# Mixing the three dilation groups inside the attention units of one hybrid decoder layer

## The chip, the cores and the metric

One Trainium2 chip, 1 core of it. The metric is device time in microseconds (us) of one launch, the median over runs. Engines: PE (matmuls), PEld (its weight loads), DVE, ACT and POOL (elementwise work), SP (issues every DMA of this kernel, in one queue, in order).

## The reference, cut to what matters

```python
def dilated_attention_branch(q, k, v):
    q, k, v = q.reshape(shp), k.reshape(shp), v.reshape(shp)   # (B, L, 3 groups, 4 heads, 128)
    for gi, (window, dilation) in enumerate(((128, 1), (512, 4), (2048, 16))):
        o, s = dilated_group_attention(q[:, :, gi], k[:, :, gi], v[:, :, gi], window, dilation)
        outs.append(o); lses.append(s)
    alpha = jax.nn.softmax(jnp.stack(lses, axis=0), axis=0)
    y = jnp.sum(alpha[..., None] * outs, axis=0)
    return y.reshape(bsz, L, ATTN_WIDTH)

def reference(x, ...):                                   # L = 2048, D_MODEL = 1024
    h = rmsnorm(x, pre_norm_g); proj = h @ w_in
    u_s, z_s, q, k, v, z_a, g_s, g_a = jnp.split(proj, SPLIT_POINTS, axis=-1)
    y_s = s5_branch(u_s, ...) * jax.nn.silu(z_s)
    y_a = dilated_attention_branch(q, k, v) * jax.nn.silu(z_a)
    merged = jax.nn.sigmoid(g_s) * (y_s @ w_branch_s) + jax.nn.sigmoid(g_a) * (y_a @ w_branch_a)
    return x + rmsnorm(merged @ w_out, post_norm_g)
```

Head slot j (0 to 3) exists in each of the three groups. Its three outputs are mixed with weights that come from the three softmax denominators.

## The kernel before, in words

The normalised input stays in SBUF as a high and a low part (`hhi`, `hlo`), and each column strip of `w_in` (128 columns) is split in the same way when it is loaded: a product is three fp32r passes, hi*hi, hi*lo and lo*hi, 24 matmuls of 512 columns for one bank of PSUM (`proj`, L141). Strips come in pairs (`pair`): four loads of 256 KB into tag `w_raw`, which has 2 buffers, and for each an ACT pass (`w_hi`, L67) and a DVE pass (`w_lo`, L68) into one of two pairs of `w_hi`/`w_lo` tiles. So the next pair can be loaded while PE works on the present one, and split when the pair before that is done with.

The stages in order: input and norm; u; the state-space branch, beside g_s, z_s and v products; its GLU; **attention**; the g_a and z_a strips; the output stage (branch products, merge, `w_out`).

Attention (`unit`) runs 12 units: head slots j = 0 to 3, and in each groups g = 0, 1, 2. A unit projects K and Q for four chunks of 512 positions. In groups 0 and 1 (`banded_chunk`) a chunk has four blocks of 128 queries against two blocks of keys (own and previous), in fp32r with high and low parts; in group 0 the last key block of a chunk is carried into the next chunk's `kh[:, 0]`, `kl[:, 0]` by two POOL copies (L848, L849). A first block without a predecessor still takes 256 columns of keys (`k0:k0+2`), and a third mask block removes the second half. Group 2 (`causal_chunk`) uses plain fp32 with 128 columns. A chunk's unnormalised output goes to DRAM (`numd`), and a unit's row maxima and sums (`statd`) follow when its last chunk is done, after a transpose (`tst`, L866).

After the last unit, `weights_of_groups` reads the statistics of each head slot, on 16 partitions, makes the three factors per position and stores them (`fd`). `combine(j)` then forms y = sum over g of factor*output for a head slot in 12 tiles of 512 positions: two loads each (`cf`: the factor row broadcast to 128 partitions; `cn`: the output), and POOL multiplies and adds. `cf` has 2 buffers, `cn` 3. Two head slots' y stay in SBUF (`cy`) and are the factor of a z_a pair (`silu_pair`). The g_a pairs (`tanh`) stand between: g_a 0-1, g_a 2-3, z_a 0-1, g_a 4-5, z_a 2-3, g_a 6-7. Each pair has 8 banks; a bank is 24 matmuls, an ACT evict into one of two `ev` buffers (`ge`, `ze`), and a store by SP (L699). A pair's weights are free to load before `combine`, from buffers of their own.

The order on each engine is made by a scheduler at build time from its own estimates; at run time every engine, and SP's queue, works strictly in that order.

Of the kernel before, what the change touches and what calls it, by code (L numbers as in the profile page):

```python
# [39 lines left out]
class Builder:  # L40
# [782 lines left out]

    def unit(self, j, g, wp, pool, ev, psum, numd, statd):
        nc = self.nc
# [4 lines left out]
        for c in range(4):  # L830
# [24 lines left out]
            else:  # L855
# [47 lines left out]
    def banded_chunk(self, g, c, carry, qh, ql, kh, kl, vh, vl, prev, st, pool, ev, psum, dst):  # L903
        nc = self.nc
        ph, pl = (pool.tile([128, 8, 128], F32R, name=n) for n in ("ph", "pl"))
        for pair in range(2):
# [3 lines left out]
            for h in range(2):  # L910
                b = 2 * pair + h
                k0 = 1 if b == 0 and not carry else b
                for n, (x, y) in enumerate(((qh, kh), (qh, kl), (ql, kh))):
                    nc.tensor.matmul(s[:, h], x[:, b], y[:, k0 : k0 + 2], start=n == 0, stop=n == 2)  # L914
            for h in range(2):
                b = 2 * pair + h
                first = b == 0 and not carry
                p = self.softmax(s[:, h], self.mask[:, 128:384] if first else self.mask[:, 0:256], 4 * c + b, st, pool)
# [29 lines left out]
        pv(nb[:, 2:4], (vh[:, 2], vl[:, 2]), 5)  # L948
        lo = pool.tile([128, 4, 128], F32, name="nlo")
        if carry:  # L950
            nc.scalar.activation(lo[:, 0:2], na[:, 0::3], AF.Copy)
        else:
            nc.scalar.activation(lo[:, 1], na[:, 3], AF.Copy)
        nc.scalar.activation(lo[:, 2:4], nb[:, 1::2], AF.Copy)
        if carry:
            nc.vector.tensor_tensor(dest[:, 0], blocks(na[:, 2:3])[:, 0], blocks(lo[:, 0:1])[:, 0], op=ALU.add)
        else:
            nc.vector.tensor_copy(dest[:, 0], blocks(na[:, 2:3])[:, 0])
        nc.vector.tensor_tensor(dest[:, 1:3], blocks(nb[:, 0::2]), blocks(lo[:, 1:3]), op=ALU.add)
        nd = psum.tile([128, 2, 128], F32, tag="n", name="nd")  # L960
        pv(nd, (vh[:, 3], vl[:, 3]), 6)
        nc.vector.tensor_tensor(dest[:, 3], blocks(nd[:, 1:2])[:, 0], blocks(lo[:, 3:4])[:, 0], op=ALU.add)
        nc.sync.dma_start(dst, acc)
# [18 lines left out]

    def weights_of_groups(self, j, pool, statd, fd):

        nc = self.nc
        m = pool.tile([16, 6, 128], F32, name="cm")
        nc.sync.dma_start(m, statd[j].rearrange("g s (r i) -> r (g s) i", r=16))
        mx = pool.tile([16, 128], F32, name="cx")
        nc.vector.tensor_tensor(mx, m[:, 0], m[:, 2], op=ALU.max)
        nc.vector.tensor_tensor(mx, mx, m[:, 4], op=ALU.max)  # L990
        e = pool.tile([16, 3, 128], F32, name="ce")
# [3 lines left out]
        t = pool.tile([16, 3, 128], F32, name="ct")  # L995
        nc.vector.tensor_tensor(t, e, m[:, 1::2], op=ALU.mult)
# [3 lines left out]
        for g in range(3):  # L1000
            nc.vector.tensor_tensor(e[:, g], e[:, g], mx, op=ALU.mult)
        nc.sync.dma_start(fd[j].rearrange("g (r i) -> r g i", r=16), e)

    def combine(self, j, pool, numd, fd):

        nc = self.nc
        y = pool.tile([128, SEQ], F32, name="cy", bufs=2)
        for q in range(4):
            qs = slice(512 * q, 512 * q + 512)
            yo = y[:, qs]  # L1010
            for g in range(3):
                f = pool.tile([128, 512], F32, name="cf", bufs=2)
                nc.sync.dma_start(f, fd[j, g : g + 1, qs].to_broadcast([128, 512]))
                n = pool.tile([128, 512], F32, name="cn", bufs=3)
                if g == 0:
                    src = numd[j, 0].rearrange("c p (h x) -> h p c x", h=4)[q]
                    nc.sync.dma_start(n.rearrange("p (c x) -> p c x", c=4), src)
                    vn = n.rearrange("p (c r i) -> p r c i", c=4, r=4)
                    vf, vy = (t.rearrange("p (r c i) -> p r c i", r=4, c=4) for t in (f, yo))
                elif g == 1:  # L1020
                    src = numd[j, 1].rearrange("c p (h x) -> h p c x", h=4)[q]
                    nc.sync.dma_start(n.rearrange("p (c x) -> p c x", c=4), src)
                    vn, vf, vy = n, f, yo
                else:
                    nc.sync.dma_start(n, numd[j, 2, q])
                    vn, vf, vy = n, f, yo
                if g == 0:
                    nc.gpsimd.tensor_tensor(vy, vn, vf, op=ALU.mult)
                else:
                    nc.gpsimd.tensor_tensor(vn, vn, vf, op=ALU.mult)  # L1030
                    nc.gpsimd.tensor_tensor(vy, vy, vn, op=ALU.add)
        return y

# [99 lines left out]
    def run(self, stop=None):  # L1133
        tc, nc, a = self.tc, self.nc, self.a
        with (
# [12 lines left out]
            statd = dp.tile([4, 3, 2, SEQ], F32, name="statd")  # L1148
            fd = dp.tile([4, 3, SEQ], F32, name="fd")
            self.vd = dp.tile([3, SEQ, 512], F32, name="vd")  # L1150
            self.ident = cst.tile([128, 128], F32, name="ident")
# [9 lines left out]
            with tc.tile_pool(name="w", bufs=2, **T) as wp, tc.tile_pool(name="ev", bufs=2, **T) as ev:  # L1161
# [37 lines left out]
                with tc.tile_pool(name="at", bufs=1, **T) as ap:  # L1199
                    self.mask = ap.tile([128, 384], F32, name="mask")  # L1200
# [4 lines left out]
                if stop == "att":  # L1205
                    return

                def emit(banks):
                    for bank in banks:
                        for step in bank:  # L1210
                            step()

                def tanh(c):
                    emit(self.tanh_pair(ev, psum, self.pair(wp, IDX_GA + c, IDX_GA + c + 1), gta[c : c + 2]))

                with tc.tile_pool(name="cb", bufs=1, **T) as cp:
                    for j in range(4):
                        self.weights_of_groups(j, cp, statd, fd)
                    for p in range(2):
                        y = [self.combine(j, cp, numd, fd) for j in (2 * p, 2 * p + 1)]  # L1220
                        if p == 0:
                            tanh(0)
                        tanh(2 + 2 * p)
                        i = IDX_ZA + 2 * p
                        emit(self.silu_pair(ev, psum, self.pair(wp, i, i + 1), ya[2 * p : 2 * p + 2], y))
                if stop == "ya":
                    return
                with tc.tile_pool(name="bs", bufs=1, **T) as bp:
                    tanh(6)
                    wb = [self.weight(bp, wp, "w_raw", n, 4, (0, 512)) for n in ("wbs", "wba")]  # L1230
# [12 lines left out]
def prepare(x, pre_norm_g, w_in, lambda_re, lambda_im, log_dt, b_re, b_im, c_re, c_im, d_skip, w_glu, b_glu,  # L1243
# [14 lines left out]
    own, before = np.where(to <= at, 0.0, NEG), np.where(to >= at, 0.0, NEG)  # L1258
    never = np.full((128, 128), NEG)
    mask = np.concatenate([before, own, never], 1)  # L1260
    diag0 = np.zeros((16, 8, 16))
# [33 lines left out]
```

## Time and profile before

| | us |
|---|---|
| median of 3 runs (2089.51 to 2094.95) | 2092.69 |
| the profiled execution's own time | 2096.55 |
| its span in the trace | 2094.7 |
| PE busy | 2049.4 (98%) |
| DVE busy | 903.0 (43%) |
| ACT busy | 592.3 (28%) |
| POOL busy | 397.8 (19%) |

PE is the engine to watch: it is busy nearly all the time, so what counts is where it is not, and where its granted clock falls from 2.4 to 1.2 GHz. The other engines matter through the waits that they cause. The times inside the span are counted from its start: attention ends near 1446 us, the g_a and z_a strips follow to about 1722 us, then the output stage.

### The profile page before, as it was taken

To read this page: it belongs to the slowest core of one execution; us is meant where nothing else is said; L and a number is where in the kernel's file an instruction comes from. 1 tells how busy PE (TensorE), PEld (TensorE's weight loads), DVE (VectorE), ACT (ScalarE), POOL (GpSimd) and SP (SyncE) were. 2 spreads that over 40 slices of the span, in tenths; PEclk is the share of its full clock that TensorE was granted. 3 is DMA by queue.
4 is the path that set the end of the run, shared out by engine and by line. 5 is a ranking of instruction groups with operands and counts; after the bars stand their busy time and mean duration, and the time that the engine had idled before them with its cause. 6 is when DMAs were issued, how large, how long until landed. Compare 5 with 4: busy or idle time off the path is not lost.

```text
span 2094.7 us, 30801 instructions
## 1 busy us (share of the span) xinstructions
PE 2049.4 (98%) x11668; PEld 1786.1 (85%) x11668; DVE 903.0 (43%) x2261; ACT 592.3 (28%) x1327; POOL 397.8 (19%) x384
## 2 busy tenths in 40 slices
PE   8999999999999999999999999999889999999998
PEld 6788888999999988888888888887777887999997
DVE  6881355555442234324424423434311226544434
ACT  6421122222223234334434333432111124112111
POOL 0002355555521200000000000001636101111111
PEclk9999999999999999999999999999999999999999
DMA  7333333333445421111111121113757246433323
GB/s 247 116 115 140 103 115 113 118 114 113 117 121 174 152 67 57 56 61 51 61 56 56 37 66 51 61 52 118 223 157 230 88 136 201 138 125 116 117 81 101
DMA packets 208372, 231.50 MB, mean 111 GB/s; under 512 B 24864, under 2 KB 142944, under 8 KB 207968
## 3 DMA queue, kind: packets, MB, share of 16 engines
q1 hardware_dynamic: 208224, 229.54, 34.9%
q8 instruction: 91, 1.49, 0.3%
q14 instruction: 57, 0.47, 0.1%
HBM read 146.52 MB, written 74.56 MB: 106 GB/s over the span
## 4 chain that ended last, share of the span: by engine, by line
PE 86%; DMA 7%; DVE 2%; ACT 1%; POOL 1%; issue 1%; SPq 0%; DVEq 0%; ACTq 0%; POOLq 0%
PE proj L141 46%; PE pv L163 13%; PE po L1108 8%; PE br L1089 8%; DMA cf<-fd 2%; PE glu L786 2%; PE s L914 2%; PE nb L940 1%; DMA raw<-in_wout_dram 1%; PE na L940 1%; PE nc L978 1%; PE py L598 1%; POOL cn L1030 1%; PE s L970 1%; PE pd L561 1%
## 5 line engine op out<-in xcount | busy, mean ns | idle before, releaser
L141 PE MATMUL proj<-hhi,w_hi 128*128 128x512 f32 x1664 | 664.6, 400 | 25.4 <-ACT ge L693 15.6
L141 PE MATMUL proj<-hlo,w_hi 128*128 128x512 f32 x1664 | 658.2, 396 | 3.3 <-DVE hlo L68 2.7
L141 PE MATMUL proj<-hhi,w_lo 128*128 128x512 f32 x1664 | 657.5, 395 | 0.0
L141 PEld LDWEIGHTS proj<-hhi,w_hi 128*128 128x128 f32 x1664 | 314.5, 189 | 95.0 <-ACT ge L693 18.4
L141 PEld LDWEIGHTS proj<-hlo,w_hi 128*128 128x128 f32 x1664 | 314.3, 189 | 71.3 <-DVE hlo L74 3.2
L141 PEld LDWEIGHTS proj<-hhi,w_lo 128*128 128x128 f32 x1664 | 314.3, 189 | 64.8
L163 PE MATMUL pv<-w_hi,hhi 128*128 128x256 f32 x768 | 218.8, 285 | 0.0
L163 PE MATMUL pv<-w_hi,hlo 128*128 128x256 f32 x768 | 214.5, 279 | 0.0
L163 PE MATMUL pv<-w_lo,hhi 128*128 128x256 f32 x768 | 214.5, 279 | 0.0
L68 DVE TENSOR_TENSOR w_lo<-w_raw,w_hi 128x512 fp32r<-128x512 f32 (+1 forms) x130 | 107.9, 854 | 195.8 <-ACT w_hi L67 195.3
L163 PEld LDWEIGHTS pv<-w_hi,hhi 128*128 128x128 f32 x768 | 144.5, 188 | 0.6
L163 PEld LDWEIGHTS pv<-w_lo,hhi 128*128 128x128 f32 x768 | 144.4, 188 | 0.6
L163 PEld LDWEIGHTS pv<-w_hi,hlo 128*128 128x128 f32 x768 | 144.4, 188 | 0.0
L898 ACT ACTIVATE p<-p,nm 128x256 f32<-128x256 f32 (+1 forms) x192 | 89.5, 467 | 151.8 <-DVE nm L897 135.7
L892 DVE CUSTOM_DVE_ANT_0 p<-s,mask 128x256 f32<-128x256 f32 (+1 forms) x192 | 68.2, 376 | 147.1 <-PE t L973 68.8
L1092 POOL TENSOR_TENSOR gt<-gt 128x256 f32<-128x256 f32 x64 | 48.7, 763 | 390.6 <-DVE gt L1091 224.7
L67 ACT ACTIVATE w_hi<-w_raw 128x512 fp32r<-128x512 f32 (+1 forms) x130 | 76.9, 620 | 111.3 <-DMA w_raw<-in_wst_dram 72.4
L848 POOL CAST kh<-kh 128x128 fp32r<-128x128 f32 x12 | 3.6, 296 | 538.2 <-PE s L970 426.3
L1108 PE MATMUL po<-wout0h,mh 128*128 128x512 f32 x256 | 99.6, 394 | 3.3 <-ACT wout0h L67 3.3
L1108 PE MATMUL po<-wout0l,mh 128*128 128x512 f32 x256 | 100.3, 392 | 0.0
L1108 PE MATMUL po<-wout0h,ml 128*128 128x512 f32 x256 | 100.2, 393 | 0.0
L693 ACT ACTIVATE ge<-proj 128x512 f32<-128x512 f32 x64 | 37.8, 594 | 205.7 <-PE proj L141 134.3
(248 smaller groups left out, 3342.1 us busy)
## 6 DMA issues: line engine op xcount, KB each, us to landing
w_raw<-in_wst_dram SPq DMA_DIRECT2D x126, 256.0 KB
vd<-ve SPq DMA_DIRECT2D x48, 256.0 KB
numd<-acc SPq DMA_DIRECT2D x48, 256.0 KB
cn<-numd SPq DMA_DIRECT2D x48, 256.0 KB
cf<-fd SPq DMA_DIRECT2D x48, 256.0 KB
xT<-in_xT_dram SPq DMA_DIRECT2D x32, 256.0 KB
gts<-ge SPq DMA_DIRECT2D x32, 256.0 KB
sx<-sx SPq DMA_DIRECT2D x64, 128.0 KB
```

Of the source, the lines that this page charges most:

```text
L67: nc.scalar.activation(hi, src, AF.Copy)
L68: nc.vector.tensor_tensor(lo, src, raw(hi), op=ALU.subtract)
L141: last = nc.tensor.matmul(ps, st[:, k, cs], m, start=n == 0, stop=n == 23)
L163: last = nc.tensor.matmul(ps[:, o], st[:, k, rs], m[:, k], start=n == 0, stop=n == 23)
L786: nc.tensor.matmul(ps, st[:, k, cs], m[:, k], start=n == 0, stop=n == 11)
L892: nc.vector.tensor_tensor_reduce(p[:, :n], scores, mask, scale=1.0, scalar=-3.0e38, op0=ALU.add, op1=ALU.max, accum_out=st[:, 0, blk : blk ...
L898: nc.scalar.activation(p[:, :n], p[:, :n], AF.Exp, scale=HEAD_SCALE, bias=nm, accum_out=st[:, 1, blk : blk + 1])
L914: nc.tensor.matmul(s[:, h], x[:, b], y[:, k0 : k0 + 2], start=n == 0, stop=n == 2)
L940: nc.tensor.matmul(out, x, y[:, i0 : i0 + 2], start=n == 0, stop=n == 2)
L1089: nc.tensor.matmul(ps, st[:, k, cs], m[:, i, k], start=n == 0, stop=n == 11)
L1092: nc.gpsimd.tensor_tensor(gt[:, 0], gt[:, 0], gt[:, 1], op=ALU.add)
L1108: nc.tensor.matmul(po[b, half], st[:, k, bs], m[:, k, hs], start=k == 0 and n == 0, stop=k == 7 and n == 2,)
```

## The change

`weights_of_groups` and `combine` become one generator per head slot (the factors now on 128 partitions x 16 positions), advanced by `next(beside)` after chunks 0, 1 and 3 of the units of the next head slot: first the factors, then 8 pieces of 256 positions. A piece has three tiles (`cnf`, one per group), each with two loads (factor and output, 128 KB each), and stores its sum to DRAM (`yad`). `cnf` is a tile of tag `w_raw`: it shares the two buffers through which all weight strips pass. Head slot 3 has no next slot; its generator is advanced after each bank of g_a 0-1 and g_a 2-3. The z_a strips read the sums back (`cy`, 3 buffers). To make room, the mask loses its third block, and a first block without a predecessor now takes 128 columns of keys; the small tile `nlo` is split in two halves.

```diff
-            if factor is not None:
-                nc.vector.tensor_tensor(e, e, factor[:, q * 512 : q * 512 + 512], op=ALU.mult)
+            if factor is not None:
+                nc.vector.tensor_tensor(e, e, factor(q), op=ALU.mult)
...
                 self.causal_chunk(c, q, k, v, st, pool, ev, psum, numd[j, g, c])
+            if c != 2:
+                next(beside, None)
...
-                k0 = 1 if b == 0 and not carry else b
+                lead = b == 0 and not carry
+                out, ks = (s[:, h, :128], slice(1, 2)) if lead else (s[:, h], slice(b, b + 2))
                 for n, (x, y) in enumerate(((qh, kh), (qh, kl), (ql, kh))):
-                    nc.tensor.matmul(s[:, h], x[:, b], y[:, k0 : k0 + 2], start=n == 0, stop=n == 2)
+                    nc.tensor.matmul(out, x[:, b], y[:, ks], start=n == 0, stop=n == 2)
...
-    def weights_of_groups(self, j, pool, statd, fd):
+    def combine(self, j, wp, pool, numd, statd, fd, yd):
-        m = pool.tile([16, 6, 128], F32, name="cm")
-        nc.sync.dma_start(m, statd[j].rearrange("g s (r i) -> r (g s) i", r=16))
+        m = pool.tile([128, 6, 16], F32, name="cm")
+        nc.sync.dma_start(m, statd[j].rearrange("g s (p x) -> p (g s) x", x=16))
...
+        nc.sync.dma_start(fd[j].rearrange("g (p x) -> p g x", x=16), e)
+        yield
         for q in range(4):
+            for o in (0, 256):
+                y = pool.tile([128, 256], F32, name="cy")
+                for g in range(3):
+                    r = wp.tile([128, 2, 256], F32, tag="w_raw", name="cnf", bufs=2)
+                    f, n = r[:, 0], r[:, 1]
+                    at = 512 * q + o
+                    nc.sync.dma_start(f, fd[j, g : g + 1, at : at + 256].to_broadcast([128, 256]))
+                    if g == 0:
+                        src = numd[j, 0].rearrange("c p (h x) -> h p c x", h=8)[2 * q + o // 256]
+                        nc.sync.dma_start(n.rearrange("p (c x) -> p c x", c=4), src)
...
+                        nc.gpsimd.tensor_tensor(vy, vn, vf, op=ALU.mult)
+                    else:
...
+                        nc.gpsimd.tensor_tensor(n, n, f, op=ALU.mult)
+                        nc.gpsimd.tensor_tensor(y, y, n, op=ALU.add)
+                nc.sync.dma_start(yd[j, q][:, o : o + 256], y)
+                yield
...
+                    beside = iter(())
                     for j in range(4):
                         for g in range(3):
-                            self.unit(j, g, wp, ap, ev, psum, numd, statd)
+                            self.unit(j, g, wp, ap, ev, psum, numd, statd, beside)
+                        beside = self.combine(j, wp, ap, numd, statd, fd, yad)
...
+                    def emit(banks, beside=iter(())):
+                        for bank in banks:
+                            for step in bank:
+                                step()
+                            next(beside, None)
+                    emit(tanh(0), beside)
+                    emit(tanh(2), beside)
+                with tc.tile_pool(name="za", bufs=1, **T) as zp:
+                    def mixed(j, q):
+                        f = zp.tile([128, 512], F32, name="cy", bufs=3)
+                        nc.sync.dma_start(f, yad[j, q])
+                        return f
                     for p in range(2):
+                        if p:
+                            emit(tanh(4))
```

How the order moves, first on SP's queue around the end of attention. Here stood, before, the weights of g_a 2-3 (`w_raw_13993`, `w_raw_13997`, their last two parts) and the first two of z_a 0-1, and only behind them the last unit's statistics and the first load of `combine`:

```order
L100 DMA w_raw_13993<-in_wst_dram 128x512
L100 DMA w_raw_13997<-in_wst_dram 128x512
L100 DMA w_raw_14227<-in_wst_dram 128x512
L100 DMA w_raw_14231<-in_wst_dram 128x512
L981 DMA numd_70<-acc_13419 128x512
L885 DMA statd_71<-stt_13520 32x128
L987 DMA cm_13527<-statd_71 16x6x128
L981 DMA numd_70<-acc_13515 128x512
L1017 DMA cn_13606<-numd_70 128x4x128
```

In the changed kernel the four parts of g_a 2-3 (`w_raw_14404` to `w_raw_14416`) stand behind the seventh of head slot 3's eight pieces (`cnf_14387`, `cnf_14391`, `cnf_14396`):

```order
L1019 DMA cnf_14387<-fd_72 128x256
L1022 DMA cnf_14387<-numd_70 128x4x64
L1034 DMA yad_73<-cy_14342 128x256
L1019 DMA cnf_14391<-fd_72 128x256
L1029 DMA cnf_14391<-numd_70 128x2x128
L1019 DMA cnf_14396<-fd_72 128x256
L1031 DMA cnf_14396<-numd_70 128x256
L100 DMA w_raw_14404<-in_wst_dram 128x512
L1034 DMA yad_73<-cy_14386 128x256
L100 DMA w_raw_14408<-in_wst_dram 128x512
L100 DMA w_raw_14412<-in_wst_dram 128x512
L100 DMA w_raw_14416<-in_wst_dram 128x512
```

So the first load of that pair moved from ahead of the mixing to behind 20 of its 24 tiles, whose buffers it needs.

The second place is POOL, in the first unit of head slot 1 (group 0). Before, it had the key carries alone:

```order
L848 COPY kh_8999<-kh_8863 128x128
L849 COPY kl_9000<-kl_8864 128x128
L848 COPY kh_9141<-kh_8999 128x128
L849 COPY kl_9142<-kl_9000 128x128
L848 COPY kh_9283<-kh_9141 128x128
L849 COPY kl_9284<-kl_9142 128x128
```

Now the last carry of that unit (`kh_9341`, `kl_9342`) stands behind the first piece and part of the second:

```order
L848 COPY kh_9197<-kh_9037 128x128
L849 COPY kl_9198<-kl_9038 128x128
L1025 TENSOR_TENSOR cy_9150<-cnf_9151 128x256
L1032 TENSOR_TENSOR cnf_9155<-cnf_9155 128x256
L1033 TENSOR_TENSOR cy_9150<-cy_9150,cnf_9155 128x256
L1032 TENSOR_TENSOR cnf_9160<-cnf_9160 128x256
L1033 TENSOR_TENSOR cy_9150<-cy_9150,cnf_9160 128x256
L1025 TENSOR_TENSOR cy_9454<-cnf_9455 128x256
L1032 TENSOR_TENSOR cnf_9459<-cnf_9459 128x256
L848 COPY kh_9341<-kh_9197 128x128
L1033 TENSOR_TENSOR cy_9454<-cy_9454,cnf_9459 128x256
L849 COPY kl_9342<-kl_9198 128x128
```

The scheduler placed seven POOL operations, each of which waits for loads, ahead of a copy that PE's scores need.

## Rows read from the trace of the kernel before

**Rows 1.** Head of the page: span, and busy time of each engine.

```profile
span 2094.7 us, 30801 instructions
PE 2049.4 (98%) x11668; PEld 1786.1 (85%) x11668; DVE 903.0 (43%) x2261; ACT 592.3 (28%) x1327; POOL 397.8 (19%) x384
```

**Rows 2.** Windows: stretch, length, busy PE, PEld, DVE, ACT, POOL; PE clock; DMA share.

```profile
1350.00:1400.00 50.00, 50.00 (x271) 42.69 (x270) 22.47 (x71) 20.21 (x56) 0.00 (x0) 1.00 0.17 54
1450.00:1500.00 50.00, 45.36 (x194) 37.09 (x193) 27.86 (x45) 6.66 (x13) 29.69 (x23) 0.97 0.68 194
```

**Rows 3.** Timeline of PE, 1276 to 1600 us: start, us, instruction, [idle before <-releaser].

```profile
1276.42 0.27 PE L866 MATMUL tst<-ident,st 128*32 128x128 f32 x1
...
1444.32 0.27 PE L866 MATMUL tst<-ident,st 128*32 128x128 f32 x1
1447.60 0.50 PE L141 MATMUL proj<-hhi,w_hi 128*128 128x512 f32 x1 [1.17 <-ACT ge L693]
...
1479.73 0.79 PE L141 MATMUL proj<-hhi,w_hi 128*128 128x512 f32 x1 [4.64 <-ACT ge L693]
1505.02 0.50 PE L141 MATMUL proj<-hhi,w_hi 128*128 128x512 f32 x1 [1.76 <-ACT ge L693]
1535.09 0.50 PE L141 MATMUL proj<-hhi,w_hi 128*128 128x512 f32 x1 [2.16 <-ACT ge L693]
1549.53 0.50 PE L141 MATMUL proj<-hhi,w_hi 128*128 128x512 f32 x1 [3.24 <-DVE ze L695]
1596.93 0.80 PE L141 MATMUL proj<-hhi,w_hi 128*128 128x512 f32 x1 [3.55 <-ACT ge L693]
```

**Rows 4.** Windows behind two of these gaps, columns as in rows 2.

```profile
1479.80:1482.60 2.80, 2.80 (x7) 2.22 (x8) 2.68 (x4) 0.36 (x1) 2.56 (x3) 0.50 0.90 301
1597.00:1602.00 5.00, 5.00 (x12) 3.95 (x13) 0.21 (x1) 0.60 (x1) 2.55 (x2) 0.50 0.76 257
```

**Rows 5.** Waits of ACT, 1445 to 1600 us: total, times, longest.

```profile
ACT ge L693 <- DMA gta<-ge: 34.9, 7, 7.3
```

**Rows 6.** Timelines of SP and of DVE from 1445 us: the factors of a head slot.

```profile
1445.42 0.34 SPq L885 DMA_DIRECT2D statd<-stt  x1
1445.86 0.36 SPq L987 DMA_DIRECT2D cm<-statd  x1
...
1447.82 0.28 DVE L989 TENSOR_TENSOR cx<-cm 16x128 f32<-16x128 f32 x1 [2.42 <-DMA cm<-statd]
1448.51 0.68 DVE L993 TENSOR_TENSOR ce<-cm,cx 16x128 f32<-16x128 f32 x3
...
1465.28 2.80 DVE L993 TENSOR_TENSOR ce<-cm,cx 16x128 f32<-16x128 f32 x3 [2.37 <-DMA fd<-ce]
```

**Rows 7.** Chain of waits, 1436 to 1500 us: start, us, what.

```profile
1447.08 2.05 DMA numd<-acc
1453.18 1.50 DMA fd<-ce
1461.85 3.34 DMA fd<-ce
1490.10 4.22 DMA cf<-fd
```

**Rows 8.** Timeline of POOL: a piece's first multiply; three pieces lie between the two.

```profile
1465.15 1.29 POOL L1028 TENSOR_TENSOR cy<-cn,cf 128x512 f32<-128x512 f32 x1
...
1494.45 1.29 POOL L1028 TENSOR_TENSOR cy<-cn,cf 128x512 f32<-128x512 f32 x1 [1.32 <-DMA cf<-fd]
```

**Rows 9.** Timelines of SP and ACT in attention: weight loads and the first split.

```profile
1258.45 5.17 SPq L100 DMA_DIRECT2D w_raw<-in_wst_dram  x4
...
1261.04 0.63 ACT L67 ACTIVATE w_hi<-w_raw 128x512 fp32r<-128x512 f32 x1 [2.33 <-DMA w_raw<-in_wst_dram]
```

**Rows 10.** Chain of waits in attention: scores of 256 columns (fp32r), of 128 (fp32).

```profile
1003.65 1.42 PE s L914 x12
...
1436.40 0.89 PE s L970 x8
```

More of the change, by code (lines that the diff above doesn't have):

```diff
@@ L822, in ordered, with unit @@
         return x
-    def unit(self, j, g, wp, pool, ev, psum, numd, statd):
+    def unit(self, j, g, wp, pool, ev, psum, numd, statd, beside):
         nc = self.nc
@@ L917, in banded_chunk @@
                 first = b == 0 and not carry
-                p = self.softmax(s[:, h], self.mask[:, 128:384] if first else self.mask[:, 0:256], 4 * c + b, st, pool)
+                if first:
+                    p = self.softmax(s[:, h, :128], self.mask[:, 128:256], 4 * c + b, st, pool)
+                else:
+                    p = self.softmax(s[:, h], self.mask, 4 * c + b, st, pool)
                 if first:
@@ L948, in banded_chunk @@
         pv(nb[:, 2:4], (vh[:, 2], vl[:, 2]), 5)
-        lo = pool.tile([128, 4, 128], F32, name="nlo")
+        lo = pool.tile([128, 2, 128], F32, name="nlo")
         if carry:
-            nc.scalar.activation(lo[:, 0:2], na[:, 0::3], AF.Copy)
+            nc.scalar.activation(lo, na[:, 0::3], AF.Copy)
+            nc.vector.tensor_tensor(dest[:, 0], blocks(na[:, 2:3])[:, 0], blocks(lo[:, 0:1])[:, 0], op=ALU.add)
         else:
             nc.scalar.activation(lo[:, 1], na[:, 3], AF.Copy)
[L954 to L957, printed above, removed]
             nc.vector.tensor_copy(dest[:, 0], blocks(na[:, 2:3])[:, 0])
-        nc.vector.tensor_tensor(dest[:, 1:3], blocks(nb[:, 0::2]), blocks(lo[:, 1:3]), op=ALU.add)
+        nc.vector.tensor_tensor(dest[:, 1], blocks(nb[:, 0:1])[:, 0], blocks(lo[:, 1:2])[:, 0], op=ALU.add)
+        lo = pool.tile([128, 2, 128], F32, name="nlo")
+        nc.scalar.activation(lo, nb[:, 1::2], AF.Copy)
+        nc.vector.tensor_tensor(dest[:, 2], blocks(nb[:, 2:3])[:, 0], blocks(lo[:, 0:1])[:, 0], op=ALU.add)
         nd = psum.tile([128, 2, 128], F32, tag="n", name="nd")
         pv(nd, (vh[:, 3], vl[:, 3]), 6)
-        nc.vector.tensor_tensor(dest[:, 3], blocks(nd[:, 1:2])[:, 0], blocks(lo[:, 3:4])[:, 0], op=ALU.add)
+        nc.vector.tensor_tensor(dest[:, 3], blocks(nd[:, 1:2])[:, 0], blocks(lo[:, 1:2])[:, 0], op=ALU.add)
         nc.sync.dma_start(dst, acc)
@@ L994, in weights_of_groups @@
         nc.scalar.activation(e, e, AF.Exp, scale=HEAD_SCALE)
-        t = pool.tile([16, 3, 128], F32, name="ct")
+        t = pool.tile([128, 3, 16], F32, name="ct")
         nc.vector.tensor_tensor(t, e, m[:, 1::2], op=ALU.mult)
@@ L1001, in weights_of_groups @@
             nc.vector.tensor_tensor(e[:, g], e[:, g], mx, op=ALU.mult)
[L1002 to L1007, printed above, removed]
+        nc.sync.dma_start(fd[j].rearrange("g (p x) -> p g x", x=16), e)
+        yield
         for q in range(4):
[L1009 to L1032, printed above, removed]
@@ L1149, in run @@
             fd = dp.tile([4, 3, SEQ], F32, name="fd")
+            yad = dp.tile([4, 4, 128, 512], F32, name="yad")
             self.vd = dp.tile([3, SEQ, 512], F32, name="vd")
@@ L1199, in run @@
                 with tc.tile_pool(name="at", bufs=1, **T) as ap:
-                    self.mask = ap.tile([128, 384], F32, name="mask")
+                    self.mask = ap.tile([128, 256], F32, name="mask")
                     nc.sync.dma_start(self.mask, a["mask"])
+                    beside = iter(())
                     for j in range(4):
                         for g in range(3):
-                            self.unit(j, g, wp, ap, ev, psum, numd, statd)
-                if stop == "att":
-                    return
@@ L1208, in emit @@
[L1208 to L1218, printed above, removed]
+                            self.unit(j, g, wp, ap, ev, psum, numd, statd, beside)
@@ new lines, in run, with tanh @@
+                        beside = self.combine(j, wp, ap, numd, statd, fd, yad)
+                    if stop == "att":
+                        return
+                    def tanh(c):
+                        w = self.pair(wp, IDX_GA + c, IDX_GA + c + 1)
+                        return self.tanh_pair(ev, psum, w, gta[c : c + 2])
+                    def emit(banks, beside=iter(())):
[3 more added lines that the diff above has]
+                            next(beside, None)
@@ L1223, in run @@
-                        tanh(2 + 2 * p)
+                        if p:
+                            emit(tanh(4))
                         i = IDX_ZA + 2 * p
-                        emit(self.silu_pair(ev, psum, self.pair(wp, i, i + 1), ya[2 * p : 2 * p + 2], y))
+                        factor = [lambda q, j=j: mixed(j, q) for j in (2 * p, 2 * p + 1)]
+                        emit(self.silu_pair(ev, psum, self.pair(wp, i, i + 1), ya[2 * p : 2 * p + 2], factor))
                 if stop == "ya":
@@ L1228, in run @@
                 with tc.tile_pool(name="bs", bufs=1, **T) as bp:
-                    tanh(6)
+                    emit(tanh(6))
                     wb = [self.weight(bp, wp, "w_raw", n, 4, (0, 512)) for n in ("wbs", "wba")]
@@ L1258, in prepare @@
     own, before = np.where(to <= at, 0.0, NEG), np.where(to >= at, 0.0, NEG)
-    never = np.full((128, 128), NEG)
-    mask = np.concatenate([before, own, never], 1)
+    mask = np.concatenate([before, own], 1)
     diag0 = np.zeros((16, 8, 16))
```

15 lines of the change are left out of this document (10 added, 5 removed).

## The prediction

> **What bounds the kernel now.** I read the head of the page first: PE is busy 98% of the span [rows 1], so time can only be won where PE stands still, or where its clock is low, or by giving it less to do. The windows show where that is: in attention PE is busy all 50 of 50 us and DMA a sixth of the time, with POOL idle; behind attention, while the groups are mixed, PE loses 4.6 of 50 us, POOL works 30 us, and DMA is at 0.68 [rows 2]. The timeline of PE gives the single stops [rows 3]. Behind most of them an ACT evict was late, and it was late because its buffer's store had not gone out [rows 5]: that store waits in SP's queue behind loads of `combine`, which wait for POOL. So the mixing does not bound anything by its length; it holds up SP's queue.
>
> **What goes.** With the mixing gone from that stretch, five stops go: 4.64 + 1.76 + 2.16 + 3.24 + 3.55 = 15.35 us [rows 3]. After two of them the granted clock is 0.50, which is the 1.2 GHz level: 19 matmuls take 7.8 us [rows 4]. Five banks of 24 ran from 1447.60 to 1479.73 - 4.64 = 1475.09, so 5.50 us a bank and 0.229 us a matmul at 2.4 GHz [rows 3]; 19 of them would be 4.35, and 3.45 us more go. The 1.17 us ahead of the first bank stay: the evict that it waits for stands where it stood. **Gain: 18.8 us.** Nothing else behind it gains: the read-back of `yad` is 16 loads with three buffers on a queue that is nearly empty by then.
>
> **What comes: a wait for the weights of g_a 2-3.** They stand on SP behind the seventh piece, in buffers that the tiles must free, and what PE has to do in the meantime is what is left of g_a 0-1. Six of its banks are left at 1447.60, as before: they end at 1447.60 + 6 x 5.50 = 1480.6.
>
> When do the weights come? First the factors. The last statistics go out at 1445.42; a small load takes 1447.82 - 1445.86 = 1.96 us [rows 6]; with the same for the store they are on chip at 1449.4. From there to the factors' store went 1453.18 - 1447.82 = 5.36 us [rows 6, 7], with rows of 128 elements; they are now 16 long. I take half, 2.7 (bounds 1.5 and 5.4), and 1.5 for the store to land (3.34 with more traffic [rows 7]): the tiles start at about 1454 (1453 to 1458).
>
> Then the tiles. Two buffers alternate: a tile's loads start when POOL is done with the tile before the last one. So two tiles take one landing X plus one tile's POOL work. On the kernel before: X = 4.22 [rows 7]; POOL 1.29 per operation [rows 8], of which three tiles have 1, 2 and 2, so 2.15 a tile; 6.37 for two, 9.6 for three. Measured: (1494.45 - 1465.15)/3 = 9.77 [rows 8], so the rule holds within 2%. Now an operation is half as wide, 0.65, and a tile 1.08. X has no row: its two loads are 256 KB together. The near end is 256 KB on a quiet queue, 1261.04 - 1258.45 = 2.59 [rows 9]; the far end is 4.22. I take 3.0, near the first, since half the bytes are asked for at about the same pace of tiles. Two tiles: 4.1 us.
>
> The first weights need the buffer of the 20th tile. The second tile ends 5.0 us after the start (an issue, X, two operations), nine pairs later is 5.0 + 36.9 = 41.9, with the 2% 42.6: 1496.6. The load takes 2.6 and ACT's split 0.63 [rows 9]: PE goes on at 1499.8. It stood 19.2 us, and the low clock after such a stop cost half of 3.45, 1.7. **Loss: 21 us.** At X = 2.59 and a start at 1453 the stop is 13 us, at 4.22 and 1458 it is 36.
>
> **The first blocks.** Their scores go from 256 to 128 columns: one block in group 0 and four in group 1 of each head slot, 20 blocks, 60 matmuls. An fp32r matmul of 256 takes 1.42/12 = 0.118 us, and four fp32 matmuls of 128 columns (two instructions each) take 0.89, so 0.222 each [rows 10]. No row shows fp32r with 128. If time goes with columns, each saves 0.059, in all -3.5; if it goes like the fp32 row, each costs 0.104 more, +6.2. I take the second: it has the same number of columns, in scores too, and only the type differs. **Loss: 6.2 us.** The smaller masks and the halved `nlo` change DVE and ACT by tenths of a microsecond off PE's path: nothing, as long as these engines keep their idle half [rows 2]; without it, some 32 additional adds would count.
>
> **Attention, slots 1 to 3.** Per slot SP issues 48 tile loads, 8 stores of y and 2 for the factors, POOL works 40 x 0.65 = 26 us, and DMA moves 24 x 256 KB and 1 MB of stores more, 7.3 MB in the 168 us from one slot's `tst` to the next [rows 3], 43 GB/s on top of 54 at a share of 0.17 [rows 2]: no bound. The order puts all eight pieces into the first 70 us of a slot, with the pair for unit 1 behind piece 2 and that for unit 2 behind piece 5. By the same count (factors 10 us after `tst`, 2.05 a tile, 3 per weight load) piece 2 ends at 23, unit 1's K parts are split near 31, and PE asks for them at 41. From 31 on eight tiles take 5.0 + 12.3, and the buffers of the split parts come free one by one, so piece 5 frees its own at 48 to 52; ACT's split of what is loaded there stands between two softmax steps of chunk 3, and PE comes to their transposes after 160 projection matmuls (37 us) and about 15 us of scores, transposes and outputs: 52 as well. The carry behind seven POOL operations is done at 21 and used at 45. So one place per slot has no margin; I take 1.3 us each. **Loss: 4 us**, between 0 and 5 us a slot (15).
>
> **Sum:** -18.8 + 21 + 6.2 + 4 = +12.4 us against the profiled execution's 2096.55. That execution was 3.9 above the median of 2092.69; the change is the same for both, so I predict 2092.7 + 12.4 = **2105 us**. Differences below 0.3% (6 us) can hardly be told from no change here.
>
> **Rivals.**
> - *The first blocks are cheap.* fp32r keeps its time per column: -18.8 + 21 - 3.5 + 4 = +2.7, so 2095, no change. For it: it is the same data type. Against it: the fp32 row at this width.
> - *POOL and the loads keep up, and it is faster.* Place: the 20 tiles behind attention. If a tile lands in 1.5 us, as the shortest transfer in rows 7 did, two tiles take 2.6 us, the 20th ends at 1454 + 3.4 + 23.2 = 1480.6, PE waits 3.2 us, and with no waits in attention the sum is -18.8 + 3.2 + 1.7 + 6.2 = -7.7: 2085. It decides from X below 1.7. Against it: a small load alone took 1.96 [rows 6].
> - *POOL holds up DVE in attention.* Three DVE subtractions took 0.68 us while POOL was idle and 2.80 beside its operations [rows 6], 0.71 more each. A slot has 12 `w_lo` and 8 `vl` splits of the same kind: 14 us of DVE; if half of it reaches PE, 7 a slot, 21 in place of 4: 2122. For it: softmax steps stand behind them in the same queue. Against it: DVE idles half of the time there [rows 2], and POOL works only a third of it.
> The Trainium skill speaks for this last rival (SBUF — State Buffer, "Who interferes with whom"): a DVE instruction with both inputs in SBUF contends with a POOL instruction that reads SBUF, and one waits for the whole of the other. The trace agrees, with 2.80 against 0.68 us; the page gives no price of its own for this kernel.
>
> **How the numbers follow.** Forecast 0.52, cheap first blocks 0.20, keeping up 0.10, DVE held up 0.18. Slower by over 0.3% are the last and most of the first: 0.60. Within 0.3%: most of the cheap blocks and the short end of the wait: 0.25. Faster: keeping up, or cheap blocks together with a stop near 13 us: 0.15. The forecast's own range, with the stop from 15 to 27 us, is 2099 to 2113; the range of 8 in 10 reaches to cheap blocks with a short stop, 2088, and to the last rival, 2122.
>
> **What would show it.** PE's timeline has one stop of 15 to 27 us between the last bank of g_a 0-1 and the first of g_a 2-3, ended by a split of `w_raw`, with 0.50 of clock behind it; the five stops of the z_a strips are gone. Scores of 128 columns start 0.2 us apart. A slot of attention takes 2 to 4 us more than the 168 of before [rows 3]. I am wrong if that stop is under 5 us, if the stops of rows 3 are still there, or if a slot takes 10 us more.

## The result, and the profile after

The changed kernel takes **2168.04 us** (median of 4 runs, 2160.6 to 2170.87), the kernel before 2091.64 (4 runs, 2089.51 to 2094.95): ratio **1.0355**, 95% interval 1.033 to 1.038. It is slower, as forecast, but by 76 us and not by 12, and outside the range. The profiled execution took 2165.62 us.

The head of the page, lines of the same kind as [rows 1]:

```profile
span 2163.8 us, 31149 instructions
PE 2062.1 (95%) x11668; PEld 1790.3 (83%) x11668; DVE 879.6 (41%) x2293; ACT 587.1 (27%) x1327; POOL 413.3 (19%) x464
```

PE has the same number of matmuls and is busy 13 us longer, in a span that is 69.1 us longer: for most of the difference it stands still. The waits of PE from slot 1 of attention to the first bank of g_a 2-3 say for whom (total, times, longest):

```profile
PE proj L141 <- ACT w_hi L67: 35.8, 1, 35.8
PE t L928 <- ACT p L900: 28.2, 16, 7.2
PE t L926 <- ACT p L900: 10.2, 3, 3.5
```

The first row is the stop that I had forecast, in the place that I had named, but 36 us long and not 19. The other two are new and lie in attention: PE is at the transposes of the softmax and ACT's exponential is late. The five stops of [rows 3] are gone. The end of each head slot, from PE's timeline, shows what this makes of a slot:

```profile
924.67 0.27 PE L868 MATMUL tst<-ident,st 128*32 128x128 f32 x1
...
1116.48 0.27 PE L868 MATMUL tst<-ident,st 128*32 128x128 f32 x1
...
1308.86 0.27 PE L868 MATMUL tst<-ident,st 128*32 128x128 f32 x1
...
1499.49 0.27 PE L868 MATMUL tst<-ident,st 128*32 128x128 f32 x1
```

The slots that have pieces beside them take 191.8, 192.4 and 190.6 us; the last took 1444.32 - 1276.42 = 167.9 before [rows 3], the two ahead of it 173.4. Where the 69.1 us are, by these marks in both traces: attention, from the first `tst` (812.43; before 815.47) to the last, 687.1 against 628.8, **+58.2** (the three slots +60.1; the rest of slot 0, which has no pieces, -1.9); behind it 664.3 against 650.4, **+13.9**; ahead of it, where nothing was changed, -3.0.

The windows after, columns as in [rows 2]: one slot, and the long stop.

```profile
1116.00:1308.00 192.00, 180.41 (x919) 149.22 (x918) 68.06 (x247) 64.08 (x177) 32.02 (x46) 0.97 0.33 89
1505.00:1575.00 70.00, 34.16 (x144) 27.88 (x143) 2.56 (x10) 5.55 (x10) 25.55 (x35) 0.74 0.50 128
```

Apart from PE no engine works much over a third of either: POOL works a sixth of a slot, and DMA is busy to a third and to a half. What is late is an order. This is the longest stop in slot 3, on PE, ACT and SP:

```profile
1373.11 0.48 PE L928 MATMUL t<-ident,p 128*128 128x128 f32 x1 [7.20 <-ACT p L900]
```

```profile
1371.93 0.63 ACT L67 ACTIVATE vh<-ev 128x512 fp32r<-128x512 f32 x1 [12.88 <-DMA ev<-vd]
```

```profile
1363.85 0.32 SPq L1019 DMA_DIRECT2D cnf<-fd  x1
1364.21 0.43 SPq L1031 DMA_DIRECT2D cnf<-numd  x1
1365.37 0.32 SPq L1019 DMA_DIRECT2D cnf<-fd  x1
1365.73 0.44 SPq L1022 DMA_DIRECT2D cnf<-numd  x1
1368.82 0.32 SPq L1034 DMA_DIRECT2D yad<-cy  x1
1369.18 0.43 SPq L100 DMA_DIRECT2D ev<-vd  x1
```

PE wants a transposed softmax; ACT's exponential for it stands in ACT's queue behind the split of the next V; ACT has waited 12.9 us for that V; and SP issued its load at 1369.18, behind the store of a piece that waited for POOL, which waited for the piece's own loads. Four queues in order, and the load at the end of the chain is a transfer of under 3 us. In ACT's waits of slots 1 to 3 this is the largest that has to do with DMA:

```profile
ACT vh L67 <- DMA ev<-vd: 88.7, 16, 12.9
ACT w_hi L67 <- DMA w_raw<-in_wst_dram: 38.3, 27, 4.6
```

Behind attention, the first multiply of the first and of the seventh piece on POOL, and the first weights of g_a 2-3 on SP and ACT:

```profile
1512.70 0.74 POOL L1025 TENSOR_TENSOR cy<-cnf 128x256 f32<-128x256 f32 x1 [99.74 <-DMA cnf<-fd]
...
1563.88 0.72 POOL L1025 TENSOR_TENSOR cy<-cnf 128x256 f32<-128x256 f32 x1 [2.08 <-DMA yad<-cy]
```

```profile
1567.97 0.33 SPq L100 DMA_DIRECT2D w_raw<-in_wst_dram  x1
```

```profile
1570.87 0.63 ACT L67 ACTIVATE w_hi<-w_raw 128x512 fp32r<-128x512 f32 x1 [31.23 <-DMA w_raw<-in_wst_dram]
```

A piece takes (1563.88 - 1512.70)/6 = 8.53 us where I had 6.15, and the weights wait for six and a half of them. At half the length a piece costs nearly what it cost before (9.77 for 512 positions [rows 8]): POOL's part halved, the landing did not.

### The profile page after: what moved, and what is told of

It reads as the page before. It is cut to its first block, busy times and chain, and to the rows that moved or that the text cites. A ratio compares the mean times of both kernels' runs of the same rounds, so it can differ in the third digit from the quotient of the medians.

```text
span 2163.8 us, 31149 instructions
## 1 busy us (share of the span) xinstructions
PE 2062.1 (95%) x11668; PEld 1790.3 (83%) x11668; DVE 879.6 (41%) x2293; ACT 587.1 (27%) x1327; POOL 413.3 (19%) x464
## 4 chain that ended last, share of the span: by engine, by line
PE 76%; DMA 13%; POOL 3%; DVE 3%; ACT 2%; issue 2%; SPq 1%; DVEq 0%; POOLq 0%; ACTq 0%
PE proj L141 40%; PE pv L163 12%; PE br L1092 7%; PE po L1111 7%; DMA cnf<-numd 4%; PE glu L786 2%; DMA w_raw<-in_wst_dram 2%; DMA yad<-cy 1%; DMA ev<-vd 1%; POOL cnf L1032 1%; DMA cnf<-fd 1%; POOL cy L1033 1%; PE s L917 1%; DMA raw<-in_wout_dram 1%; PE py L598 1%
## 5 line engine op out<-in xcount | busy, mean ns | idle before, releaser
L900 ACT ACTIVATE p<-p,nm 128x128 f32<-128x128 f32 (+1 forms) x192 | 87.2, 455 | 170.7 <-DVE nm L899 170.4
L894 DVE CUSTOM_DVE_ANT_0 p<-s,mask 128x128 f32<-128x128 f32 (+1 forms) x192 | 64.8, 361 | 105.0 <-PE t L980 40.7
L1094 DVE SCALAR_TENSOR_TENSOR gt<-gt,br 128x256 f32<-128x256 f32 x128 | 51.8, 418 | 68.9 <-PE br L1092 38.9
```

Of the source, the lines that this page charges most:

```text
L894: nc.vector.tensor_tensor_reduce(p[:, :n], scores, mask, scale=1.0, scalar=-3.0e38, op0=ALU.add, op1=ALU.max, accum_out=st[:, 0, blk : blk ...
L900: nc.scalar.activation(p[:, :n], p[:, :n], AF.Exp, scale=HEAD_SCALE, bias=nm, accum_out=st[:, 1, blk : blk + 1])
L1094: nc.vector.scalar_tensor_tensor(gt[:, i], gt[:, i], 1.0, ps, op0=ALU.add, op1=ALU.mult)
```

## The experiments

Twelve kernels ran, each in 5 rounds against the kernel before, whose median was 2094.12 beside the first four, 2096.55 beside the next four and 2091.42 beside the last four. Theory S: SP's queue, in which V, weights and stores stand behind pieces. Rivals: the pieces' own pace (their one `cy` buffer), the two buffers that pieces and weights share (theory R), and POOL against DVE.

**first128.** The kernel before, with only the scores and the softmax of the first blocks at 128 columns.

```diff
-                k0 = 1 if b == 0 and not carry else b
+                lead = b == 0 and not carry
+                out, ks = (s[:, h, :128], slice(1, 2)) if lead else (s[:, h], slice(b, b + 2))
...
+                if first:
+                    p = self.softmax(s[:, h, :128], self.mask[:, 128:256], 4 * c + b, st, pool)
```

> The kernel before with the first blocks alone changed (scores and softmax of 128 columns). If an fp32r matmul goes with its columns: 60 x 0.06 = 3.6 us less than the kernel before, about 2088. If it costs as much as the fp32 row of this width: 6.2 us more, about 2098.

Measured: 2095.52, ratio 1.0007 (0.9999 to 1.0016): neither. PE's timeline at such a block (start, us):

```profile
1004.96 0.23 PE L915 MATMUL s<-kh,qh 128*128 128x128 f32 x1
1005.02 0.28 PE L915 MATMUL s<-kl,qh 128*128 128x128 f32 x1
1005.13 0.33 PE L915 MATMUL s<-kh,qh 128*128 128x256 f32 x1
1005.30 0.22 PE L915 MATMUL s<-kh,ql 128*128 128x128 f32 x1
1005.36 0.33 PE L915 MATMUL s<-kh,qh 128*128 128x256 f32 x1
1005.53 0.28 PE L915 MATMUL s<-kl,qh 128*128 128x256 f32 x1
```

A matmul of 128 columns gives way to the next after 0.06 to 0.11 us, but the ones of 256 that follow take 0.17 until the next start, where they take 0.12 elsewhere. I read it as the next weights, for whose loading the short one leaves too little time, so that what it saves is given back. The weight loads of these matmuls bear it out: they start 0.11 to 0.13 us apart, beside short matmuls as beside long ones.

```profile
1004.96 0.19 PEld L915 LDWEIGHTS s<-kl,qh 128*128 128x128 f32 x1
1005.07 0.19 PEld L915 LDWEIGHTS s<-kh,qh 128*128 128x128 f32 x1
1005.18 0.19 PEld L915 LDWEIGHTS s<-kh,ql 128*128 128x128 f32 x1
```

The Trainium skill says the like (TensorE: Matmul & The Clock Gate, "Back-to-back issue gap"): the spacing is set by weight load and matmul together, and the matmul's own time counts too little at 128 columns. The rows of fp32r agree in that, with 0.11 to 0.13 us from weight load to weight load. From the first `tst` to the last, attention took 627.9 us against 628.8.

**ahead.** The weights of g_a 2-3 are asked for ahead of the last slot's pieces.

```diff
-                    emit(tanh(0), beside)
-                    emit(tanh(2), beside)
+                    banks = [tanh(0), tanh(2)]
+                    emit(banks[0], beside)
+                    emit(banks[1], beside)
```

> The changed kernel with the weights of g_a 2-3 asked for ahead of the last slot's pieces. If the long stop is those weights standing behind the pieces in SP's queue, the stop of 36 us goes with the 5 us of half clock behind it, attention stays as slow as it was, and the time is 2168 - 41 = 2127 (2122 to 2135). If the pieces are too slow wherever the weights stand, the stop comes back at g_a 4-5 or z_a 0-1 and less than half is gained: above 2148.

Measured: 2151.79, ratio 1.0282 (1.0268 to 1.0295): between the two. The long stop is gone, and three others came, 2.1, 3.5 and 13.1 us from start to start, at the evicts of g_a 2-3:

```profile
PE proj L141 <- ACT ge L693: 18.7, 4, 12.7
```

The stores of these evicts, next in line behind the pieces, are late in its place; `tailfix` below shows that SP's queue is not all of it.

**vfirst.** Each piece is begun behind the next chunk's V load.

```diff
                 self.load_split(ev, "ev", vh, vl, vsrc)
+                if c != 3 and (c or g):
+                    next(beside, None)
...
-            if c != 2:
-                next(beside, None)
+        if g == 2:
+            next(beside, None)
```

(in the unbanded chunks likewise, behind the load of `v`)

> The changed kernel with each piece issued behind the next chunk's V load instead of ahead of it. If the stops of attention are V loads that stand behind a piece in SP's queue, and ACT's split of V in front of the exponentials: a slot goes from 191 to about 178 us, three slots give back 35 to 40 us, the long stop in front of g_a 2-3 stays, and the time is about 2130 (2125 to 2142). If POOL holds up DVE, or the pieces' pace is what PE waits for, the slots stay near 191 and the time above 2155.

Measured: 2175.16, ratio 1.0388 (1.0373 to 1.0404): above 2155, with slots of 193.8, 193.8 and 191.1, but no clean test of either theory. In the order that SP got, the five V loads that come among the pieces stand behind 5, 13, 23, 35 and 47 of a slot's tile loads, where they stood behind 6, 13, 25, 33 and 44: V hardly moved, and the weights of the next two units went out 9 to 10 us earlier in the slot. PE waited for other things and as long:

```profile
PE nd L950 <- DVE acc L963: 16.0, 3, 5.8
PE t L930 <- ACT p L904: 12.8, 3, 4.5
```

**cy2.** Two buffers for a piece's sum.

```diff
-                y = pool.tile([128, 256], F32, name="cy")
+                y = pool.tile([128, 256], F32, name="cy", bufs=2)
```

(`cm`, `cx`, `ce` and `ct` become one tile in the buffer of `nlo`, for room.)

> The changed kernel with two buffers for a piece's sum (the factors' small tiles share the buffer of nlo, to make room). If the piece's store is what slows the pieces: 8.5 us a piece goes to 6.2, the long stop from 36 to about 20, and attention gives back a part of its stops with it: 2135 (2125 to 2150). If the loads' own landing sets the pace, a piece stays above 8 and the time above 2160.

Measured: 2197.13, ratio 1.0496 (1.0482 to 1.0509). The tail answers the question, on POOL from the first piece to the seventh:

```profile
1541.09 0.74 POOL L1024 TENSOR_TENSOR cy<-cnf 128x256 f32<-128x256 f32 x1 [89.65 <-issue]
...
1591.57 0.72 POOL L1024 TENSOR_TENSOR cy<-cnf 128x256 f32<-128x256 f32 x1 [1.99 <-DMA cnf<-fd]
```

(1591.57 - 1541.09)/6 = 8.41 us a piece: the store's wait was gone, the loads' wait took its place, and the stop stayed at 35 us. That attention became 24 us slower than in the changed kernel (711.0 against 687.1) may have to do with the borrowed buffer, or with the order that it makes; no run shows which.

**poolq.** All DMAs of the pieces go out from POOL's own queue; nothing else changes in the source.

```diff
-                    nc.sync.dma_start(f, fd[j, g : g + 1, at : at + 256].to_broadcast([128, 256]))
+                    nc.gpsimd.dma_start(f, fd[j, g : g + 1, at : at + 256].to_broadcast([128, 256]))
...
-                nc.sync.dma_start(yd[j, q][:, o : o + 256], y)
+                nc.gpsimd.dma_start(yd[j, q][:, o : o + 256], y)
```

> The changed kernel with every load and store of the pieces issued from POOL's own queue instead of SP's; buffers and their sharing with the weights stay. If PE's stops in attention come from SP's queue, in which V, the weights and the stores of acc stand behind pieces: a slot goes from 191 to 178 us or less, and the weights of g_a 2-3 come sooner; 2168 - 45 = about 2123 (2100 to 2140). If the two buffers that pieces and weights share are the cause, the stops stay and the time is above 2155.

Measured: 2124.98, ratio 1.0135 (1.0118 to 1.0153). This one decides for attention. Its waits of PE, from the first slot to behind g_a 2-3, and a window of one slot:

```profile
PE proj L141 <- ACT w_hi L67: 48.8, 1, 48.8
PE proj L141 <- ACT ge L693: 1.2, 1, 1.2
```

```profile
1101.00:1274.00 173.00, 173.00 (x920) 146.16 (x918) 70.05 (x247) 65.64 (x177) 65.58 (x102) 1.00 0.38 99
```

Every stop in attention is gone, at full clock; it takes 628.6 us, as before the change (628.8), with the same pieces, the same shared buffers, more bytes a second than in the changed kernel, and POOL beside DVE. So neither theory R by itself nor POOL against DVE costs attention anything; the pieces' place in SP's queue costs it 58 us. Two things this run does not part from it. The scheduler also made a somewhat different order on PE and ACT: in slot 2, half of PE's 920 instructions keep their place and nine in ten move by 8 places or fewer. And no run has the pieces of slots 1 to 3 on SP's queue with buffers of their own. The Trainium skill says (DMA: Bandwidth & Descriptors, "Issuing engines are not separate DMA queues") that issuing from several engines saves only the time that it takes to initiate a DMA, usually little. The runs differ: what was saved is not the initiating (0.3 to 0.5 us each on SP) but the waits that stand ahead of a load in its queue.

The long stop, however, grew to 49, where I had expected the weights sooner. SP, with no piece in its queue, waited ahead of these loads, which need the tiles' buffers, and what came last was a tile's load:

```profile
SPq L100 <- DMA cnf<-fd: 42.4, 1, 42.4
```

**poolqahead.** Both edits, that of `poolq` and that of `ahead`.

> As the one before, and the weights of g_a 2-3 asked for ahead of the last slot's pieces. If SP's queue is the cause of both kinds of stop, the long stop goes too: about 2087 (2075 to 2110), below the kernel before. If the shared buffers are the cause, above 2135.

Measured: 2098.68, ratio 1.0005 (0.9995 to 1.0014): inside the range, but level with the kernel before and not below it. The wait for weights came back one pair later, 18.8 us:

```profile
PE proj L141 <- ACT w_hi L67: 18.8, 1, 18.8
```

These loads are on SP, where no piece stands in front of them any more; SP waited for a tile (12.8 us, `SPq L100 <- DMA cnf<-numd`) ahead of them. Behind attention theory R holds: the weights take turns with the tiles in two buffers.

**poolqvh.** `poolq`, and the last slot's tiles in the buffers of `vh`, which attention needs no longer by then.

```diff
+                    if j < 3:
                         r = wp.tile([128, 2, 256], F32, tag="w_raw", name="cnf", bufs=2)
+                    else:
+                        r = pool.tile([128, 4, 128], F32, tag="vh", name="cnf", bufs=2)
```

> The changed kernel with the pieces' DMAs on POOL's queue, and the last slot's tiles in the two buffers of vh, which attention no longer needs, instead of those shared with the weights. If what is left of the long stop (49.1 us with POOL's queue alone, 19.2 with the weights asked for first) is the shared buffers, it goes with the half clock behind it: 2125 - 49 - 3 = 2073 (2068 to 2082), faster than both kernels. If it comes from the landing of the pieces or a queue, above 2095.

Measured: **2078.06, ratio 0.9933 (0.9921 to 0.9945)**, as expected and faster than both. PE's largest wait is 5.3 us, once, for a z strip's factor:

```profile
PE proj L141 <- DVE ze L695: 5.3, 1, 5.3
```

**tailvh.** The same edit of the buffers as in `poolqvh`, with all DMAs on SP's queue.

> The changed kernel, all on SP's queue, with only the last slot's tiles in the buffers of vh. If in the kernel as changed SP's queue alone holds the weights of g_a 2-3 back, the stop stays at 36 us: 2160 to 2172. If the shared buffers did, it falls by half or more: below 2150.

Measured: 2136.45, ratio 1.0215 (1.0201 to 1.0229), below 2150: the stop for weights is gone, an evict's stop of 9.3 us is there instead. I had taken the order on SP for given. It is not: with buffers of their own the weights moved ahead of the pieces on SP by themselves (the four loads stand in front of the last slot's first load, where they stood in its seventh piece). Sharing buffers had set the order of the queue.

**vq.** Only the V loads go to POOL's queue.

```diff
-            self.nc.sync.dma_start(r, src[sl])
+            (self.nc.gpsimd if tag == "ev" else self.nc.sync).dma_start(r, src[sl])
...
-                nc.sync.dma_start(v, vsrc)
+                nc.gpsimd.dma_start(v, vsrc)
```

> The changed kernel with only the V loads of attention issued from POOL's queue; pieces, weights and stores of acc stay on SP. If V alone makes attention's stops (14 of 16 end in ACT's split of V), a slot goes from 191 to 178 us, and the time to 2168 - 38 = 2130 (2122 to 2140). If weights and carries are as late as V, the next of them takes the place: slots of 184 and more, above 2148.

Measured: 2151.12, ratio 1.0286 (1.0272 to 1.0301): the second alternative. Attention took 675.5, so V alone gives back 11.6 of 58. The weights of the next unit are late next, and K's split stands behind theirs on ACT; SP's queue shows them among the pieces:

```profile
984.38 0.32 SPq L1019 DMA_DIRECT2D cnf<-fd  x1
984.74 0.43 SPq L1031 DMA_DIRECT2D cnf<-numd  x1
988.59 0.33 SPq L100 DMA_DIRECT2D w_raw<-in_wst_dram  x1
990.07 0.32 SPq L1034 DMA_DIRECT2D yad<-cy  x1
990.43 0.43 SPq L970 DMA_DIRECT2D numd<-acc  x1
```

**actstore** and **tailfix.** The stores of the g_a strips go out from ACT's queue, in the kernel before and in `ahead`.

```diff
-        return product, evict, lambda: nc.sync.dma_start(dst[q], t["e"])
+        return product, evict, lambda: (nc.sync if silu else self.gq).dma_start(dst[q], t["e"])
```

> The kernel before with the stores of its g_a strips issued from ACT's queue instead of SP's. If its five stops are stores that stand behind the combine's loads in SP's queue: 12 to 18 of their 17.3 us (five gaps from start to start) go, and some of the half clock: 2094 - 15 = 2079 (2074 to 2084). If the evicts wait for something else (the DMA engines, busy to 0.68), the time stays above 2088.

> The changed kernel with the weights of g_a 2-3 asked for first, and the stores of g_a from ACT's queue. If the three stops of 2.1, 3.5 and 13.1 us that the first alone left are these stores behind pieces in SP's queue: 18.7 us and the half clock's 6.8 go from its 2152: about 2127. If not, the time stays above 2142.

Measured: 2092.52, ratio 0.9980 (0.9971 to 0.9989), and 2148.22, ratio 1.0249 (1.0232 to 1.0266): the second alternative in both, with little gained: 4 us in the first; in the second 4 by the times, 7 by the two ratios. Leaving SP's queue did not help the stores, since ACT is a queue too. In `tailfix` ACT's evicts still wait for landings of the pieces:

```profile
1565.68 0.33 ACTq L699 DMA_DIRECT2D gta<-ge  x1
1566.11 0.60 ACT L693 ACTIVATE ge<-proj 128x512 f32<-128x512 f32 x1 [10.52 <-DMA cnf<-numd]
```

In the program's order some of ACT's stores wait for counts of landed DMAs that loads on SP add to as well (eight counts, each of 1 to 6 DMAs from ACT and 153 to 158 from SP); I take it that they wait for their turn there, which no run of its own tested. In the kernel before, two of the five stops are not late stores: ahead of the stop of 4.64 us ACT waits, in order, for the factors of a later slot, and ahead of that of 1.76 for weights:

```profile
1478.68 0.52 ACT L994 ACTIVATE ce<-ce 16x384 f32<-16x384 f32 x1 [9.52 <-DVE ce L993]
1503.14 1.34 ACT L67 ACTIVATE w_hi<-w_raw 128x512 fp32r<-128x512 f32 x2 [9.99 <-DMA w_raw<-in_wst_dram]
```

In `actstore` the same two are 4.7 and 5.5 us long from start to start. The expectation below takes both for waits for factors; the second is the one for weights.

**beforeq.** The kernel before, with the loads of `combine` (factors and sums) from POOL's queue.

```diff
-                nc.sync.dma_start(f, fd[j, g : g + 1, qs].to_broadcast([128, 512]))
+                nc.gpsimd.dma_start(f, fd[j, g : g + 1, qs].to_broadcast([128, 512]))
```

(and the three loads of `n` alike)

> The kernel before with the loads of combine (factors and sums) issued from POOL's queue instead of SP's. If the five stops (17.3 us) are stores of g_a held up by these loads, in SP's queue or by the counts that DMAs of both queues share, they go but for those in which ACT waits in order for DVE's factors (4.7 and 5.5 us when the stores were moved): 2096 - 8 = 2088 (2080 to 2091). If POOL, which now issues its own loads, becomes late with y for the z strips, 2096 or more.

Measured: **2074.86, ratio 0.9925 (0.9910 to 0.9939)**, better than I expected: 18.8 us of waits became 5.1, and no half clock is left there, so 16.6 us went. Of what is left, 3.0 us is again ACT's wait for `ce`. Four edited lines give what the change was after, with no pieces at all.

```profile
PE proj L141 <- ACT ge L693: 4.2, 2, 3.0
PE proj L141 <- DVE ze L695: 0.9, 1, 0.9
```

## Why the prediction was right in its sign, and wrong in its size and about attention

- **The sign** is not luck: behind attention, where the forecast had its mechanism right, the kernel is slower by 13.9 us, without what attention adds. By the prediction's own last sign it is wrong all the same, since a slot takes 18 to 23 us more.
- **The gain of 18.8 us** is right: the stops of [rows 3] are gone. That they were stores behind SP's loads [rows 5] was only partly so: `beforeq` frees most of it, but one stop came through ACT's wait for `ce` and one through ACT's wait for weights.
- **The wait for g_a 2-3's weights, +21.** Mechanism and place were right (`tailvh`, `ahead`), the size was not: 36 us and 2.1 of clock, 38. The term that was mis-sized is X, the landing of a tile's two loads, "I take 3.0, near the first". Two tiles take 8.53 x 2/3 = 5.69 us, of which POOL has 5 x 0.73/3 = 1.22: X is 4.47, beyond even my far end of 4.22 [rows 7]. That is a remainder: from the first issue of a tile's loads to POOL's start on it went 3.5 to 5.1 us, 4.3 on average over 21 tiles, and in 6 of them what landed last was the store of the sum before. "Half the bytes" was no reason: a landing hardly shortens with them here. The Trainium skill has the like for the DMAs that POOL issues (DMA: Bandwidth & Descriptors, "Anatomy of one DMA — SWDGE (gpsimd) path"): some 2.0 us of a DMA do not depend on its size. Its fit gives 2.3 us for 128 KB and 2.6 for 256 KB, an estimate by that page, which is not for SP's queue; two loads there took more in both kernels, but the small difference between the sizes agrees. The start was right (the first multiply came 13.2 us behind `tst`; my count gives 9.7 and X). Nine pairs at 5.69 instead of 4.1 are 14.3 of the 16.6 us by which the weights came later than I had them. The 36 us that the prediction gives as its far end has a late start in it, which did not come. (By its own terms a stop of 15 us gives 2101, not the 2099 at the low end of its range.)
- **The first blocks, +6.2.** Wrong, and so was the rival's -3.5: 128 columns are as cheap as their columns say, but the matmul behind them gives it back. Nearly 0.
- **Attention, +4.** This is the step that failed: "So one place per slot has no margin; I take 1.3 us each". It was about 20 a slot. I had counted 2.05 us a tile where it was 2.84, and with what stands between them the pieces are in SP's queue for some 90 us of a slot, not 70; and I had compared only the weights and the carry with the time at which PE wants them. The eight V loads of a slot's banded chunks stand in the same queue, and ACT's split of V stands ahead of exponentials; I did not look at them. 38.4 us are waits of PE; seven stretches at 0.50 clock, 30.7 us together with PE at work for 25.0, cost 12.5 more; some 7 us I have no term for. The bound of 5 us a slot had no row behind it.
- **The rival POOL against DVE.** Slots became slower by more than its 7 us, but by another mechanism. The splits `vl` took 0.738 us on average (0.692 before), 0.840 in `poolq`, where POOL works while PE never waits. Only those that met a multiply or add of POOL took longer: 8 of 24 with 0.83 us, in `poolq` 10 of 24 with 1.05; the others, and all `w_lo` splits, none of which met one, stayed at 0.69. So the contention that the Trainium skill describes (SBUF — State Buffer, "Who interferes with whom") shows in the durations, with 0.4 us of DVE a slot and 1.2 in `poolq` where the rival had 14, and in `poolq` it costs PE nothing.
- **Keeping up** was excluded by X.

Sum by the terms as measured: attention with the first blocks +58.2 where I had 10.2; behind it +13.9 where I had 2.2. The terms give 38 - 18.8 = 19.2 there: 5 us more went than I have terms for, 1.7 of them with a third stretch of half clock of the kernel before (1769.6 to 1773.0 us).

## What to carry to other kernels

Before work is put "beside" other work, list every load and store that shares an in-order queue with it, not only those that are known to be tight, and price the piece by its landing, which did not halve with its size. A load that waits for a slow consumer belongs on a queue whose later entries depend on nobody else, here the consumer's own: that alone gave 0.9925 on the kernel before, and 0.9933 on the changed kernel together with buffers of its own. When one entry was taken out of the blocked queue or moved ahead in it, the next one took its place (`ahead`, `vq`).

## What was not expected of the hardware

- An fp32r matmul of 128 columns gives way after 0.06 to 0.11 us, but 0.17 us pass behind the next one of 256 in place of 0.12.
- A piece of 256 positions took 8.5 us and one of 512 took 9.8, with the bytes of every load halved.
- POOL issuing its own DMAs took 0.54 to 0.75 us of POOL for each (busy 65.6 us a slot against 32), SP some 0.4; with room on POOL that was free.
- At the longest stop PE's clock was at 0.50 (1.2 GHz) for 37.5 us, 32.8 of them with PE idle, so that only 4.6 us of work ran at the low level:

```profile
1538.70:1571.50 32.80, 0.00 (x0) 0.00 (x0) 0.00 (x0) 1.23 (x2) 14.46 (x20) 0.50 0.49 127
1571.60:1576.20 4.60, 4.60 (x11) 3.63 (x12) 1.69 (x3) 1.26 (x2) 0.00 (x0) 0.50 0.44 121
```
